# TensorE's order in a linear recurrence, written out for six of its eight pairs of heads

## The chip, the cores and the metric

The kernel runs on one core of a Trainium2 chip, as one program of some 42,600 instructions. The metric is the device time of one execution in microseconds; the table below has three timed runs and the profiled one. A core has five engines that are used here: TensorE (matmuls and transposes), VectorE, ScalarE, GpSimd and SyncE (which issues most transfers). Each goes through its own list of instructions in the order in which they were put there and waits on semaphores for the others.

## The reference

Three blocks of a network run one after the other on 512 tokens of width 1024: two attention layers, a block with a recurrence (RWKV) and a gated convolution, and a block with mLSTM and differential attention. All is in single precision; the kernel does each large matmul as three, from the high and low halves of both operands. The change lies in the second block:

```python
proj = h @ w_in                       # 1024 x 6400: r, k, v, low ranks, conv, gates
def step(S, inp):                     # one token; 16 heads of 64
    r_t, w_t, k_t, v_t, a_t, b_t = inp
    sa = einsum('bhij,bhj->bhi', S, a_t)
    S = S * w_t[:, :, None, :] + sa[..., None] * b_t[:, :, None, :] + v_t[..., None] * k_t[:, :, None, :]
    return S, einsum('bhij,bhj->bhi', S, r_t)
...
kk = kk / maximum(sqrt(sum(kk * kk)), 1e-12)      # per head
y = _rwkv7_scan(rh, decay, kh, vh, -kk, kk * ah)
y = (y - mean(y)) * rsqrt(var(y) + GN_EPS)        # per head
y_b = silu(layer_norm(conv1d(glu, conv_w, width 31) + conv_b))
merged = concatenate([(y + bonus) * g, y_b]) * sigmoid(gates)
x = x + gt_m * (merged @ w_out)
```

## The kernel before

`block2` is the second block. The 16 heads are worked in eight **pairs**, each on 128 partitions, and the 512 tokens in eight **chunks** of 64. For each pair p there are three parts.

`rwkv_prep` makes the operands: the low-rank decay and gates (`ps_w`, `ps_a`, `ps_cum`), the projections r, k, v (72 matmuls of 128x512 into `psg`, evicted as `xs_k`, `xs_r`, `xs_v`), the norm of each key column (`ps_kn`, the value `n`, an rsqrt by Newton steps on VectorE, `ps_kt`), then `kk`, `ar`, `kE`, the products within a chunk (`ps_M`, masked into four `MLR`) and transposes (`ps_kb`, `ps_vt`, `ps_bon`).

`rwkv_invert` inverts the triangular matrices of the chunks. Its 32x32 blocks go through DRAM to another layout (`dram_L`, then `uL`), VectorE inverts them in some 35 dependent steps (`uM`, `uT`, `uX`), the result comes back through DRAM (`dram_DT`, then `zD`), and TensorE puts the halves together (`ps_D`, `ps_T`, `ps_X`); ScalarE copies to `zD` and `XO` last.

`rwkv_steps` is the **chain** over the eight chunks. A chunk has three **hops** on TensorE: `ps_P<-S,ar` (copied by ScalarE to `VY`), the two `ps_u` (copied to `VU`), and `ps_s`, after which VectorE updates the state S in two instructions; two `ps_P<-VU,MLR` for the next chunk follow. Then come the outputs (16 `ps_y`), a normalisation per head on VectorE, GpSimd and ScalarE (GN), four transposes `ps_yt`, and Y goes to DRAM.

Beside that stand the **fillers**: the column tiles of the convolution (`conv_tiles`: matmuls, `glu`, and 30 **taps** on VectorE for each of eight tiles, into `z0` to `z7`) and of the gates (`gate_tiles`: matmuls and a sigmoid). Each column tile is 24 matmuls. A list `order` says which fillers are issued behind which pair: "c12" is convolution tiles 1 and 2, "g02" gate tiles 0 and 1.

The program is written in this order: prep and invert of pair 0; then for each pair its chain, prep and invert of the next pair, and the fillers of that pair at a lower priority. A scheduler lays out each engine's list from priorities and dependencies. Two lines bind it besides: the matmul `from_v` of a chunk comes after the last one of the chunk before, and the first tap of a convolution tile comes after the last step of the inversion that was issued last before the tile:

```python
inv = self.inv_last               # conv_tiles, when it is called
...
if j == 1:
    self.issue_after(tap, inv)
```

PSUM has four banks for `psg`, two for the preparation, and one each for `ps_u`/`ps_s` and `ps_P`. Weights come in slabs, which ScalarE rounds to their high half (`whi`) and VectorE or GpSimd subtract to the low half (`wlo`); in this stage one slab in three goes to VectorE.

## Time and profile before

| | |
|---|---|
| timed runs | 3638.11, 3644.20, 3645.26 us, median 3644.2 |
| profiled execution, its own time | 3647.22 us |
| its span, first to last instruction | 3645.4 us |
| mean granted TensorE clock | 0.929 |
| busy in the span: TensorE | 3261.1 us (89%) |
| VectorE | 2078.6 us (57%) |
| ScalarE | 1321.2 us (36%) |
| GpSimd | 522.7 us (14%) |

A share of busy time is a mean over stages with different limits. The granted clock is a share of 2.4 GHz; 0.5 is the lower of its two levels, 1.2 GHz. "Idle before" is how long an engine stood before an instruction, with what ended the wait.

### The profile page before, as it was taken

To read this page: it belongs to the slowest core of one execution; us is meant where nothing else is said; L and a number is where in the kernel's file an instruction comes from. 1 tells how busy PE (TensorE), PEld (TensorE's weight loads), DVE (VectorE), ACT (ScalarE), POOL (GpSimd) and SP (SyncE) were. 2 spreads that over 40 slices of the span, in tenths; PEclk is the share of its full clock that TensorE was granted. 3 is DMA by queue.
4 is the path that set the end of the run, shared out by engine and by line. 5 is a ranking of instruction groups with operands and counts; after the bars stand their busy time and mean duration, and the time that the engine had idled before them with its cause. 6 is when DMAs were issued, how large, how long until landed. Compare 5 with 4: busy or idle time off the path is not lost. (4 is left out here: it accounts for less than half of the span.)

```text
span 3645.4 us, 42576 instructions
## 1 busy us (share of the span) xinstructions
PE 3261.1 (89%) x15209; PEld 2559.2 (70%) x15209; DVE 2078.6 (57%) x3962; ACT 1321.2 (36%) x2472; POOL 522.7 (14%) x623
## 2 busy tenths in 40 slices
PE   8999999999999996785847766789999999999998
PEld 6666777887788875563635555678887777788887
DVE  4576654646653565665653834743336775566565
ACT  3465322334432342231222212433324454344344
POOL 1000010111110111220211212321101001101011
PEclk9999999999999997895866867899999999999999
DMA  4313554352233331110210213323333323433232
GB/s 145 97 58 99 160 163 139 125 144 74 78 98 98 99 103 42 54 53 14 61 40 26 59 40 119 107 85 98 95 97 90 102 64 110 144 99 99 93 95 84
DMA packets 275286, 332.64 MB, mean 91 GB/s; under 512 B 53212, under 2 KB 188314, under 8 KB 275073
## 3 DMA queue, kind: packets, MB, share of 16 engines
q1 hardware_dynamic: 237392, 301.43, 27.1%
q0 software_dynamic: 3936, 16.03, 1.4%
q10 hardware_dynamic: 33745, 12.46, 1.4%
q8 instruction: 120, 1.97, 0.2%
q14 instruction: 93, 0.76, 0.1%
HBM read 311.94 MB, written 23.89 MB: 92 GB/s over the span
## 5 line engine op out<-in xcount | busy, mean ns | idle before, releaser
L123 PE MATMUL psg<-hhi,whi 128*128 128x512 f32 (+1 forms) x2624 | 1049.3, 402 | 59.5 <-DVE glu L1318 27.4
L118 DVE TENSOR_TENSOR wlo<-raw,whi 128x512 fp32r<-128x512 f32 (+2 forms) x865 | 628.6, 738 | 795.2 <-PE psg L124 422.0
L125 PE MATMUL psg<-hhi,wlo 128*128 128x512 f32 (+1 forms) x2624 | 1046.3, 400 | 28.6 <-POOL wlo L118 15.5
L124 PE MATMUL psg<-hlo,whi 128*128 128x512 f32 (+1 forms) x2624 | 1047.5, 399 | 0.0
L117 ACT CAST whi<-raw 128x512 fp32r<-128x512 f32 (+2 forms) x975 | 582.6, 604 | 1196.1 <-PE psg L124 1031.3
L123 PEld LDWEIGHTS psg<-hhi,whi 128*128 128x128 f32 (+1 forms) x2624 | 500.9, 191 | 182.9 <-issue 29.4
L125 PEld LDWEIGHTS psg<-hhi,wlo 128*128 128x128 f32 (+1 forms) x2624 | 501.2, 191 | 141.4 <-POOL wlo L118 19.5
L124 PEld LDWEIGHTS psg<-hlo,whi 128*128 128x128 f32 (+1 forms) x2624 | 502.0, 191 | 104.7 <-issue 1.7
L123 PE MATMUL psg<-hidhi,whi 128*128 128x512 f32 x784 | 308.8, 394 | 2.1 <-DVE ffg L574 1.2
L125 PE MATMUL psg<-hidhi,wlo 128*128 128x512 f32 x784 | 307.5, 392 | 0.0
L124 PE MATMUL psg<-hidlo,whi 128*128 128x512 f32 x784 | 306.1, 390 | 0.0
L1322 DVE SCALAR_TENSOR_TENSOR z<-glu,par_B,z 128x512 f32<-128x512 f32 x240 | 185.2, 800 | 3.3
L118 POOL TENSOR_TENSOR wlo<-raw,whi 128x512 fp32r<-128x512 f32 (+1 forms) x110 | 139.0, 1272 | 286.7 <-ACT whi L117 202.8
L125 PEld LDWEIGHTS psg<-hidhi,wlo 128*128 128x128 f32 x784 | 147.2, 188 | 34.3
L123 PEld LDWEIGHTS psg<-hidhi,whi 128*128 128x128 f32 x784 | 147.4, 188 | 34.0 <-issue 1.6
L124 PEld LDWEIGHTS psg<-hidlo,whi 128*128 128x128 f32 x784 | 147.3, 188 | 32.9
L581 POOL TENSOR_TENSOR ffu<-ffu,ffg 128x512 f32<-128x512 f32 x44 | 64.6, 1469 | 587.9 <-DVE ffu L574 587.9
L1273 DVE SCALAR_TENSOR_TENSOR S<-S,GC,ps_s 64x64 f32<-64x64 f32 x112 | 31.3, 280 | 130.0 <-PE ps_s L1271 128.5
L1391 POOL TENSOR_TENSOR ffr<-ffr 128x512 f32<-128x512 f32 x32 | 40.1, 1261 | 293.8 <-ACT ffr L1390 288.9
L1212 PE MATMUL ps_D<-ident,zD 128*128 128x128 f32 x32 | 7.9, 394 | 82.0 <-DMA zD<-dram_DT 82.0
L194 ACT CAST hidhi<-ffu 128x512 fp32r<-128x512 f32 x66 | 41.0, 622 | 106.1 <-POOL ffu L581 66.2
L195 DVE TENSOR_TENSOR hidlo<-ffu,hidhi 128x512 fp32r<-128x512 f32 x66 | 57.3, 868 | 30.9 <-ACT hidhi L194 29.4
(576 smaller groups left out, 4174.8 us busy)
## 6 DMA issues: line engine op xcount, KB each, us to landing
raw<-in_ffn_w_gu_dram SPq DMA_DIRECT2D x176, 256.0 KB
raw<-in_w_in_dram SPq DMA_DIRECT2D x59, 512.0 KB
adraw<-in_ada_w_dram SPq DMA_DIRECT2D x48, 512.0 KB
raw<-in_w_up_dram SPq DMA_DIRECT2D x88, 256.0 KB
raw<-in_ffn_w_down_dram SPq DMA_DIRECT2D x42, 512.0 KB
raw<-in_w_ff_in_dram SPq DMA_DIRECT2D x32, 512.0 KB
...
```

Of the source, the lines that this page charges most:

```text
L117: nc.scalar.copy(oi(hi), ri(r))
L118: eng.tensor_tensor(out=oi(lo), in0=ri(r), in1=fr(oi(hi)), op=ALU.subtract)
L123: first = nc.tensor.matmul(ps, lhsT=whi, rhs=xhi, start=start, stop=False)
L124: nc.tensor.matmul(ps, lhsT=whi, rhs=xlo, start=False, stop=False)
L125: nc.tensor.matmul(ps, lhsT=wlo, rhs=xhi, start=False, stop=stop)
L194: nc.scalar.copy(hi, t)
L195: nc.vector.tensor_tensor(out=lo, in0=t, in1=fr(hi), op=ALU.subtract)
L581: nc.gpsimd.tensor_tensor(out=t, in0=t, in1=part[c], op=ALU.mult)
L1212: nc.tensor.transpose(ps[:, c * 128:(c + 1) * 128], DT[:, 2 * c:2 * c + 2, :].rearrange("p c t -> p (c t)"), self.ident)
L1273: nc.vector.scalar_tensor_tensor(out=S[h, h], in0=S[h, h], scalar=GC[h, c:c + 1], in1=pss[h, h], op0=ALU.mult, op1=ALU.add)
L1322: tap = nc.vector.scalar_tensor_tensor(out=z[i], in0=g[:, j:j + T], scalar=cw(j), in1=z[i], op0=ALU.mult, op1=ALU.add)
L1391: nc.gpsimd.tensor_tensor(out=t, in0=t, in1=t, op=ALU.mult)
```

## The change

Matmuls and transposes go through two helpers, `mm` and `tp`, which record them in named segments. The order of issue in `block2` is another: `rwkv_prep` is cut in two (the first half is `ps_w` to the projections, the second the rest), `rwkv_steps` in three (chain; outputs and GN; `ps_yt`), all as generators. For pair p now come the chain of p, the outputs of p-1, the second half of the preparation of p+1, the `ps_yt` of p-1, the fillers of p, the first half of the preparation of p+2, and the inversion of p+1. For pairs 0 to 5 `in_turn` then gives TensorE's order in full: it lists fillers and preparation in a fixed sequence, gives each matmul a weight, and puts the 24 hops of the chain in at equal distances in these weights. All recorded matmuls behind pair 5 come after the end of that list. VectorE, ScalarE, GpSimd and the transfers keep the scheduler's order. Fillers are spread anew over the pairs, `VY` gets a second buffer, and `bon` lies in other buffers.

```diff
-            order = ["c01", "c12", "c31 g02", "c42", "g22", "c62 g41", "g51 h01", "g62 h13 n h44 x p y04 n2 q r y43 m08 s", "x yw y7 w"]
+            order = ["c01 g02", "c12", "c31 g22", "c42", "c61 g42", "c71 g62", "h04", "n h44 x p y04 n2 q r y43 m08 s", "x yw y7 w"]
...
-            P = self.rwkv_prep(W, act, 0, low)
-            self.rwkv_invert(P)
-            for f in order[0].split():
-                filler(f)
-            for p in range(8):
-                low["y7"] = self.rwkv_steps(P, y_d)
-                if p < 7:
-                    P = self.rwkv_prep(W, act, p + 1, low)
-                    self.rwkv_invert(P)
+            def fill(p):
+                self.seg("F", p)
                 for f in order[p + 1].split():
                     filler(f)
+            prep = {p: self.rwkv_prep(W, act, p, low) for p in range(8)}
+            next(prep[0])
+            P = next(prep[0])
+            next(prep[1])
+            self.rwkv_invert(P)
+            fill(-1)
+            end, steps = None, {}
+            for p in range(8):
+                steps[p] = self.rwkv_steps(P, y_d)
+                for q in {6: (6, 5, 5, 6, 6), 7: (7, 7, 7)}.get(p, (p, p - 1)):
+                    if q >= 0:
+                        low["y7"] = next(steps[q])
+                if p < 7:
+                    P = next(prep[p + 1])
+                if 0 < p < 6:
+                    next(steps[p - 1])
+                fill(p)
+                if p < 6:
+                    next(prep[p + 2])
+                if p < 7:
+                    self.rwkv_invert(P)
+                if p < 6:
+                    end = self.in_turn(p, end)
...
+    def in_turn(self, p, end):
+        g = lambda *n: [(i, {"w": 0.25, "G": 0.23, "F": 0.23, "kn": 0.12, "kt": 0.11, "M": 0.1, "D": 0.11, "T": 0.06, "X": 0.06,
+                             "y": 0.1, "yt": 0.1}[n[0]]) for i in self.segs.get(n, [])]
+        F, G = g("F", p), g("G", p + 2)
+        cut = lambda l, us: (l[:int(us / 0.23)], l[int(us / 0.23):])
+        f0, F = cut(F, 1.5)
+        f1, F = cut(F, 4.0)
+        f2, F = cut(F, 8.0)
+        f3, F = cut(F, 4.0)
+        G, g2 = G[:-14], G[-14:]
+        B = (g("y", p - 1) + f0 + g("kn", p + 1) + f1 + g("kt", p + 1) + f2 + g("M", p + 1) + f3 + g("yt", p - 1) + F + g("w", p + 2) + G +
+             g("D", p + 1) + g2[:7] + g("T", p + 1) + g2[7:] + g("X", p + 1))
+        step = sum(w for _, w in B) / 24
+        out, t, k = [], 0.0, 0
+        for i, w in B:
+            while k < 24 and t >= step * k:
+                out += self.segs.get(("C", p, k), [])
+                k += 1
+            out.append(i)
+            t += w
...
+        for a, b in zip(([end] if end is not None else []) + out, out if end is not None else out[1:]):
+            self.issue_after(b, a)
+        return out[-1]
```

What this moves, first on TensorE around the `ps_D` of the second preparation. Rows are line, operation, output and inputs, size; `hhi` and `hlo` are the activations' halves, and the number of `zD` tells even and odd pairs apart (10969 is an odd pair's). Before:

```order
L124 MATMUL psg<-hlo_10768,whi 128x512
L125 MATMUL psg<-hhi_10767,wlo 128x512
L123 MATMUL psg<-hhi_10773,whi 128x512
L1212 MATMUL ps_D<-ident,zD_10969 128x128 x4
L124 MATMUL psg<-hlo_10774,whi 128x512
L125 MATMUL psg<-hhi_10773,wlo 128x512
L123 MATMUL psg<-hhi_10779,whi 128x512
L1218 MATMUL ps_T<-D,zC 32x32 x16
L124 MATMUL psg<-hlo_10780,whi 128x512
L125 MATMUL psg<-hhi_10779,wlo 128x512
L123 MATMUL psg<-hhi_10785,whi 128x512
L1226 MATMUL ps_X<-zD_10969,zT 32x32 x16
```

Before, `ps_D`, `ps_T` and `ps_X` of a pair (here pair 1) stand among fillers, and no hop of a chain lies between them. After, around the `ps_D` of pair 2:

```order
L130 MATMUL ps_P<-S,ar 128x128
L130 MATMUL psg<-hhi_10797,wlo 128x512
L130 MATMUL psg<-hhi_10803,whi 128x512
L136 MATMUL ps_D<-ident,zD_10968 128x128 x4
L130 MATMUL psg<-hlo_10804,whi 128x512
L130 MATMUL psg<-hhi_10803,wlo 128x512
L130 MATMUL psg<-hhi_10797,whi 128x512
L130 MATMUL psg<-hlo_10798,whi 128x512
L130 MATMUL psg<-hhi_10797,wlo 128x512
L130 MATMUL ps_u<-VY,zD_10969 64x64
L130 MATMUL ps_u<-VY,XO 64x64
L130 MATMUL psg<-hhi_10803,whi 128x512
```

The `psg` here are projections of pair 3, and hops of the chain of pair 1 (`ps_P<-S,ar`, then `ps_u` from `zD_10969`) stand before and behind the `ps_D` of pair 2.

The second place is the start of a preparation on TensorE. Before, behind the chain of pair 1:

```order
L123 MATMUL psg<-hhi_10779,whi 128x512
L1298 MATMUL ps_yt<-ident,Y 128x128 x4
L1054 MATMUL ps_w<-WD,tw 128x128 x4
L124 MATMUL psg<-hlo_10780,whi 128x512
L125 MATMUL psg<-hhi_10779,wlo 128x512
L123 MATMUL psg<-hhi_10785,whi 128x512
L1059 MATMUL ps_a<-alo,WA 128x512
L1064 MATMUL ps_cum<-tri,sT 128x128 x4
```

After the transposes of pair 1's output come `ps_w`, `ps_a` and `ps_cum` of pair 2, and its projections follow. After, behind the last step (`ps_X`) of pair 2's preparation:

```order
L130 MATMUL ps_P<-VU,MLR 128x64
L130 MATMUL ps_P<-S,ar 128x128
L130 MATMUL ps_y<-VU,MLR 64x64 x16
L130 MATMUL psg<-hhi_10761,whi 128x512
L130 MATMUL psg<-hlo_10762,whi 128x512
L130 MATMUL psg<-hhi_10761,wlo 128x512
L130 MATMUL ps_u<-VY,XO 64x64
L130 MATMUL ps_u<-VY,zD_10968 64x64
L130 MATMUL psg<-hhi_10767,whi 128x512
L130 MATMUL psg<-hlo_10768,whi 128x512
L130 MATMUL psg<-hhi_10767,wlo 128x512
L130 MATMUL ps_kn<-bones,kksq 128x2 x4
```

The chain of pair 2 begins, the outputs of pair 1 and six fillers with a hop between follow, and then `ps_kn` of pair 3; `ps_w` and the projections of pair 3 have stood ahead.

The third is VectorE in the last steps of an inversion. Before, of pair 1; `z_10973` and `z_10974` are the convolution's tiles 1 and 2, so rows with them are taps:

```order
L1173 TENSOR_REDUCE uX<-uT 128x6x8
L1172 TENSOR_TENSOR uT<-uX,uL 128x384
L1173 TENSOR_REDUCE uX<-uT 128x2x8
L1172 TENSOR_TENSOR uT<-uX,uL 128x256
L1173 TENSOR_REDUCE uX<-uT 128x2x8
L1172 TENSOR_TENSOR uT<-uX,uL 128x128
L1173 TENSOR_REDUCE uX<-uT 128x2x8
L1172 TENSOR_TENSOR uT<-uX,uM 128x512
L1173 TENSOR_REDUCE uX<-uT 128x8x8
L1322 SCALAR_TENSOR_TENSOR z_10973<-glu,par_B,z_10973 128x512
L118 TENSOR_TENSOR wlo<-raw,whi 128x384
L1322 SCALAR_TENSOR_TENSOR z_10973<-glu,par_B,z_10973 128x512 x6
```

The steps follow each other, and the taps stand behind the last. After, in the inversion of pair 2, with the taps of tile 3 (L1248 and L1249 are the steps that were L1172 and L1173):

```order
L1248 TENSOR_TENSOR uT<-uX,uM 128x384
L1409 SCALAR_TENSOR_TENSOR z_10975<-glu,par_B,z_10975 128x512
L1249 TENSOR_REDUCE uX<-uT 128x6x8
L1409 SCALAR_TENSOR_TENSOR z_10975<-glu,par_B,z_10975 128x512
L1248 TENSOR_TENSOR uT<-uX,uL 128x384
L1409 SCALAR_TENSOR_TENSOR z_10975<-glu,par_B,z_10975 128x512
L1249 TENSOR_REDUCE uX<-uT 128x2x8
L1409 SCALAR_TENSOR_TENSOR z_10975<-glu,par_B,z_10975 128x512
L1248 TENSOR_TENSOR uT<-uX,uL 128x256
L1356 SCALAR_TENSOR_TENSOR S<-S,GC,ps_s 64x64 x2
L1249 TENSOR_REDUCE uX<-uT 128x2x8
```

Each step has a tap behind it.

## Rows read from the trace of the kernel before

**Rows 1.** The page's slices: busy tenths of TensorE, and the TensorE clock granted, in 40 equal slices of 91.1 us; the sixteenth slice begins at 1367 us.

```profile
PE   8999999999999996785847766789999999999998
...
PEclk9999999999999997895866867899999999999999
```

**Rows 2.** Busy time of each engine in stretches: start:end and length, then busy us of TensorE's matmuls, its weight loads, VectorE, ScalarE and GpSimd (instructions in brackets), the mean granted clock, the busy share of the DMA engines, GB/s. The first is the recurrence, the second runs from the first ps_u of pair 0 to that of pair 6, the third from that of pair 7 to the next block's ps_sum.

```profile
1360.00:2320.00 960.00, 663.29 (x3534) 506.71 (x3533) 548.63 (x1083) 252.16 (x515) 183.56 (x234) 0.77 0.19 55
...
1434.57:2155.55 720.98, 486.86 (x2652) 374.62 (x2652) 422.91 (x832) 184.05 (x377) 141.93 (x189) 0.77 0.16 44
...
2286.42:2423.63 137.21, 116.12 (x521) 91.05 (x521) 85.29 (x138) 48.72 (x88) 50.72 (x37) 0.86 0.31 96
...
2320.00:2350.00 30.00, 15.37 (x84) 12.01 (x83) 29.66 (x42) 15.04 (x23) 22.18 (x15) 0.74 0.31 98
```

**Rows 3.** TensorE in order of time, start and duration in us; in brackets the idle time before it and what ended it: the first ps_u of pair 0; the steps of pair 1's preparation; the first ps_u of pair 1; the first of pair 6.

```profile
1434.57 0.33 PE L1267 MATMUL ps_u<-VY,XO 64*64 64x64 f32 x2 [1.14 <-ACT XO L1232]
...
1472.33 1.11 PE L1298 MATMUL ps_yt<-ident,Y 128*128 128x128 f32 x4 [8.47 <-POOL Y L1295]
...
1481.22 1.05 PE L1084 MATMUL ps_kn<-bones,kksq 128*128 128x2 f32 x8 [1.70 <-ACT kksq L1081]
...
1547.52 1.05 PE L1212 MATMUL ps_D<-ident,zD 128*128 128x128 f32 x4
...
1551.45 1.10 PE L1226 MATMUL ps_X<-zD,zT 128*32 128x32 f32 x32
...
1553.84 0.32 PE L1267 MATMUL ps_u<-VY,XO 64*64 64x64 f32 x2
...
2155.55 0.47 PE L1267 MATMUL ps_u<-VY,XO 64*64 64x64 f32 x2 [1.14 <-ACT XO L1232]
```

**Rows 4.** VectorE in order of time in the same preparation, of pair 1: the column norm (n), its use (kk), the four MLR, the inversion's first step (uM) and last (uX).

```profile
1482.31 0.17 DVE L1087 TENSOR_SCALAR n<-ps_kn 128x8 f32<-128x8 f32 x1 [0.17 <-PE ps_kn L1084]
...
1490.07 0.69 DVE L1097 TENSOR_TENSOR kk<-kk,ps_kt 128x512 f32<-128x512 f32 x1 [1.45 <-PE ps_kt L1096]
...
1496.31 1.29 DVE L1117 TENSOR_TENSOR MLR<-ps_M,maskM 128x512 f32<-128x512 f32 x2 [1.31 <-PE ps_M L1114]
...
1498.64 1.29 DVE L1117 TENSOR_TENSOR MLR<-ps_M,maskM 128x512 f32<-128x512 f32 x2 [1.04 <-PE ps_M L1114]
...
1515.63 1.13 DVE L1178 COPY uM<-uL 128x256 f32<-128x256 f32 x1 [6.85 <-POOL uL L1162]
...
1532.24 0.69 DVE L1173 TENSOR_REDUCE uX<-uT 128x64 f32<-128x512 f32 x1
```

**Rows 5.** Who waited for whom in 1360 to 2320 us: us in total, times, longest.

```profile
PE ps_D L1212 <- DMA zD<-dram_DT: 82.0, 5, 29.7
...
PE ps_yt L1298 <- POOL Y L1295: 69.9, 7, 17.7
...
PE ps_P L1262 <- DVE S L1273: 9.3, 25, 1.1
...
DVE uM L1178 <- POOL uL L1162: 65.6, 8, 10.0
```

**Rows 6.** TensorE in order of time: two matmuls of the projections, 128x512, that follow each other at the lower clock, and two at the full one; the distance of their starts is what one costs.

```profile
1586.73 0.63 PE L125 MATMUL psg<-hhi,wlo 128*128 128x512 f32 x1
...
1587.15 0.63 PE L123 MATMUL psg<-hhi,whi 128*128 128x512 f32 x1
...
1591.31 0.40 PE L123 MATMUL psg<-hhi,whi 128*128 128x512 f32 x1
...
1591.54 0.39 PE L124 MATMUL psg<-hlo,whi 128*128 128x512 f32 x1
```

**Rows 7.** TensorE and VectorE in order of time, other pairs: ps_D of pair 0; the last uX and the ps_D of pair 2; ps_w and ps_kn, the last uX and the ps_D of pair 7.

```profile
1428.07 1.09 PE L1212 MATMUL ps_D<-ident,zD 128*128 128x128 f32 x4 [7.53 <-DMA zD<-dram_DT]
...
1659.02 0.69 DVE L1173 TENSOR_REDUCE uX<-uT 128x64 f32<-128x512 f32 x1
...
1667.84 1.09 PE L1212 MATMUL ps_D<-ident,zD 128*128 128x128 f32 x4 [29.08 <-DMA zD<-dram_DT]
...
2195.19 1.91 PE L1054 MATMUL ps_w<-WD,tw 128*128 128x128 f32 x8
...
2202.70 1.05 PE L1084 MATMUL ps_kn<-bones,kksq 128*128 128x2 f32 x8 [2.08 <-ACT kksq L1081]
...
2262.92 0.69 DVE L1173 TENSOR_REDUCE uX<-uT 128x64 f32<-128x512 f32 x1
...
2279.32 0.76 PE L1212 MATMUL ps_D<-ident,zD 128*128 128x128 f32 x4
```

**Rows 8.** VectorE's groups by line in 1360 to 2320 us (count | busy us, mean ns | idle before, and whom it waited for): the taps of the convolution and the update of the state. The mean of a tap counts pieces twice that overlap; 185.2 us for 240 is 0.77.

```profile
L1322 DVE SCALAR_TENSOR_TENSOR z<-glu,par_B,z 128x512 f32<-128x512 f32 x240 | 185.2, 800 | 3.3
...
L1273 DVE SCALAR_TENSOR_TENSOR S<-S,GC,ps_s 64x64 f32<-64x64 f32 x112 | 31.3, 280 | 130.0 <-PE ps_s L1271 128.5
```

**Rows 9.** VectorE in order of time: two steps of small rsqrt chains on 128x4 and 128x8, the first beside an idle GpSimd, the second while the convolution is normalised.

```profile
2318.46 0.16 DVE L255 TENSOR_TENSOR rs_t<-rs_t,rs_h 128x4 f32<-128x4 f32 x1
...
2341.39 1.23 DVE L255 TENSOR_TENSOR rs_t<-rs_t,rs_h 128x8 f32<-128x8 f32 x1
```

**Rows 10.** TensorE in order of time in pair 7's chain: the first ps_u of two chunks that follow each other with no filler between.

```profile
2290.47 0.47 PE L1267 MATMUL ps_u<-VY,zD 64*64 64x64 f32 x2 [0.35 <-ACT VY L1263]
...
2294.57 0.47 PE L1267 MATMUL ps_u<-VY,XO 64*64 64x64 f32 x2 [0.35 <-ACT VY L1263]
```

More of the change, by code (lines that the diff above doesn't have):

```diff
@@ L122, in mm3, with mm, tp, seg @@
         nc = self.nc
-        first = nc.tensor.matmul(ps, lhsT=whi, rhs=xhi, start=start, stop=False)
-        nc.tensor.matmul(ps, lhsT=whi, rhs=xlo, start=False, stop=False)
-        nc.tensor.matmul(ps, lhsT=wlo, rhs=xhi, start=False, stop=stop)
-        return first
+        first = self.mm(ps, lhsT=whi, rhs=xhi, start=start, stop=False)
+        self.mm(ps, lhsT=whi, rhs=xlo, start=False, stop=False)
+        self.mm(ps, lhsT=wlo, rhs=xhi, start=False, stop=stop)
+        return first
+    def mm(self, *a, **k):
+        i = self.nc.tensor.matmul(*a, **k)
+        if self.rec is not None:
+            self.rec.append(i)
+        return i
+    def tp(self, *a, **k):
+        i = self.nc.tensor.transpose(*a, **k)
+        if self.rec is not None:
+            self.rec.append(i)
+        return i
+    def seg(self, *name):
+        self.rec = None if name == (None,) else self.segs.setdefault(name, [])
     def issue_after(self, ins, earlier):
@@ L234, in colsum @@
                 first = i == 0 and b == 0
-                self.sum_ins = nc.tensor.matmul(ps[:, 0:8] if first else ps[:, b * 2:b * 2 + 2],
+                self.sum_ins = self.mm(ps[:, 0:8] if first else ps[:, b * 2:b * 2 + 2],
                                                 lhsT=ss[:, b * 128:(b + 1) * 128],
@@ L395, in toeplitz_table @@
             ps = self.ps("s", "ps_t")
-            nc.tensor.matmul(ps[0:nh, 0:w], lhsT=t, rhs=oh, start=True, stop=True)
+            self.mm(ps[0:nh, 0:w], lhsT=t, rhs=oh, start=True, stop=True)
             nc.vector.scalar_tensor_tensor(out=o, in0=ps[0:nh, 0:w], scalar=-1.0, in1=ad, op0=ALU.mult, op1=ALU.subtract)
@@ L480, in sc @@
                 def sc(e, qb, ps):
-                    nc.tensor.matmul(ps, lhsT=qz[2 * m + e][:, qb * 128:(qb + 1) * 128], rhs=kt[m], start=True, stop=True)
+                    self.mm(ps, lhsT=qz[2 * m + e][:, qb * 128:(qb + 1) * 128], rhs=kt[m], start=True, stop=True)
                 po = self.ps("o", "ps_pv")
@@ L542, in sc @@
                 def sc(e, qb, ps):
-                    nc.tensor.matmul(ps, lhsT=qh[2 * m + e][:, qb * 128:(qb + 1) * 128], rhs=kh[2 * m + e], start=True, stop=True)
+                    self.mm(ps, lhsT=qh[2 * m + e][:, qb * 128:(qb + 1) * 128], rhs=kh[2 * m + e], start=True, stop=True)
                 po = self.ps("o", "ps_pv")
@@ new lines, in block2 @@
+            self.lo_on = "v"
+            self.seg(None)
+            late = [i for n, l in self.segs.items() for i in l if (n[0] in ("C", "F") and n[1] > 5) or (n[0] in ("y", "yt") and n[1] >= 5)
+                    or (n[0] in ("kn", "kt", "M", "D", "T", "X") and n[1] > 6)]
+            for i in late:
+                self.issue_after(i, end)
+            rst.close()
+    def in_turn(self, p, end):
[18 more added lines that the diff above has]
+            t += w
+        while k < 24:
+            out += self.segs.get(("C", p, k), [])
+            k += 1
+        for a, b in zip(([end] if end is not None else []) + out, out if end is not None else out[1:]):
+            self.issue_after(b, a)
+        return out[-1]
@@ L1050, in rwkv_prep @@
         got = {}
+        self.seg("w", p)
         ps = self.psp("ps_w")
         for b in range(NB):
-            nc.tensor.matmul(ps[:, b * 128:(b + 1) * 128], lhsT=low["w"][:, b * 128:(b + 1) * 128], rhs=WD,
+            self.mm(ps[:, b * 128:(b + 1) * 128], lhsT=low["w"][:, b * 128:(b + 1) * 128], rhs=WD,
                              start=True, stop=True)
@@ L1058, in rwkv_prep @@
         ps = self.psp("ps_a")
-        nc.tensor.matmul(ps, lhsT=WA, rhs=low["a"], start=True, stop=True)
+        self.mm(ps, lhsT=WA, rhs=low["a"], start=True, stop=True)
         at = self.rot("a")
@@ L1077, in rwkv_prep @@
         r, k, v = got["r"], got["k"], got["v"]
+        yield
+        self.seg("kn", p)
         kk = self.rot("kk")
@@ L1141, in rwkv_prep @@
         ps = self.psp("ps_bon")
-        nc.tensor.matmul(ps, lhsT=self.bones, rhs=t, start=True, stop=True)
-        bon = self.sp.tile([128, T], F32, tag="RSTD", name="bon", bufs=2) if p % 3 == 2 else self.rp.tile([128, T], F32, tag="bon", name="bon", bufs=2)
+        self.mm(ps, lhsT=self.bones, rhs=t, start=True, stop=True)
+        bon = self.sp.tile([128, T], F32, tag="RSTD", name="bon", bufs=2) if p % 3 else self.rp.tile([128, T], F32, tag="bon", name="bon")
         nc.vector.tensor_tensor(out=bon, in0=ps, in1=v, op=ALU.mult)
-        return dict(p=p, Ld=Ld, ar=arc, KB=KB, VU=VU, MLR=MLR, MLRc=MLRc, GC=GC, bon=bon)
+        yield dict(p=p, Ld=Ld, ar=arc, KB=KB, VU=VU, MLR=MLR, MLRc=MLRc, GC=GC, bon=bon)
     def cdma(self, **kw):
@@ L1257, in from_v @@
                 self.issue_after(i, last[0])
-            nc.tensor.matmul(psP[:, c % 4, up], lhsT=MLRc[:, 1, c], rhs=VU[:, c, up], start=False, stop=False)
+            self.mm(psP[:, c % 4, up], lhsT=MLRc[:, 1, c], rhs=VU[:, c, up], start=False, stop=False)
+        self.seg("C", p, 0)
         from_v(0)
         for c in range(8):
-            last[0] = nc.tensor.matmul(psP[:, c % 4, :], lhsT=ar[:, c], rhs=S, start=False, stop=True)
+            self.seg("C", p, 3 * c)
+            last[0] = self.mm(psP[:, c % 4, :], lhsT=ar[:, c], rhs=S, start=False, stop=True)
             nc.scalar.copy(VY[:, c, :], psP[:, c % 4, :])
             own = halves[1 - c % 2]
+            self.seg("C", p, 3 * c + 1)
             psu = self.ps("st", "ps_u")
             for e, h in enumerate(halves):
-                nc.tensor.matmul(psu[up, h], lhsT=XT(e, c), rhs=VY[own, c, h], start=True, stop=True)
+                self.mm(psu[up, h], lhsT=XT(e, c), rhs=VY[own, c, h], start=True, stop=True)
             nc.scalar.copy(VU[up, c, :], psu[up, 0:128])
+            self.seg("C", p, 3 * c + 2)
             if c < 7:
                 pss = self.ps("st", "ps_s")
-                nc.tensor.matmul(pss[:, 0:128], lhsT=KB[:, c, :], rhs=VU[:, c, :], start=True, stop=True)
+                self.mm(pss[:, 0:128], lhsT=KB[:, c, :], rhs=VU[:, c, :], start=True, stop=True)
                 for h in halves:
@@ L1279, in rwkv_steps @@
                 for q in range(2):
-                    nc.tensor.matmul(psy[halves[q], b, h], lhsT=MLR[up, e, b, 3 * q, :], rhs=VU[up, 2 * b + q, h], start=True, stop=True)
+                    self.mm(psy[halves[q], b, h], lhsT=MLR[up, e, b, 3 * q, :], rhs=VU[up, 2 * b + q, h], start=True, stop=True)
         for q, h in enumerate(halves):
```

83 lines of the change are left out of this document (47 added, 36 removed).

## The prediction

> **What bounds the kernel now.** I read the slices of the page first: TensorE is full almost everywhere but in a dip of ten slices, where its granted clock falls too [rows 1]. The stretches say how large the dip is: 1360 to 2320 us, 960 us, in which TensorE is busy 663 us at a mean clock of 0.77, VectorE 549 us, and no other engine half as long [rows 2]. No engine bounds this stage; a loop does. Its period is read from the first ps_u of each pair's chain: 1434.57 for pair 0, 2155.55 for pair 6, so 721.0 us for six pairs, 120.2 us each [rows 3].
>
> One round of the loop, from pair 0 to pair 1, read from the instructions of VectorE and TensorE in order of time [rows 3, 4]: chain and its output 1434.6 to 1472.3 (ps_yt), projections from there to 1481.2 (ps_kn), then the column norm, n at 1482.31 to kk at 1490.07 (7.8 us), kk to the first MLR 6.2, the four MLR to 1499.93 (3.6), a trip through DRAM to uM at 1515.63 (15.7), the inversion to the end of the last uX, 1532.93 (17.3), a second trip to ps_D at 1547.52 (14.6), ps_D to the end of ps_X 5.0, and the next chain at 1553.84. All of it is one after the other: the chain of pair p, then the preparation of p+1. Who waits confirms it: TensorE stands 82.0 us before ps_D and 69.9 us before ps_yt, and the inversion's start on VectorE, uM, waits 65.6 us in eight pairs for uL [rows 5]. The big matmuls ("fillers") that stand behind ps_D and ps_yt on TensorE wait with them.
>
> **The change part by part.** *Wrapping matmuls in a helper, recording them:* no instruction. *The order for pairs 0 to 5:* the chain of pair p now runs beside the preparation of p+1, hop by hop, and the projections of p+2 fill the time before ps_D. This removes from the loop the chain, GN and projections, 1434.6 to 1481.2, 46.6 us a round. What is left, X to X: end of ps_X to the norm, with the 16 ps_y, a few fillers and ps_kn ahead of it, 5 us (1.3 us to the first ps_u in [rows 3, 4], 1.1 for ps_kn, the rest fillers); norm 8; kk to MLR 11, since 34 fillers of 0.23 us [rows 6] and two hops now stand before ps_M; MLR 3.6; first trip 17 (15.7 here, where uM waited 6.85 us; the mean wait is 65.6 / 8 = 8.2 [rows 4, 5]); inversion 17; second trip 8.5 (14.6 and 15.7 where TensorE came late, 8.1 where ps_D itself waited for the transfer [rows 4, 7]); D to X 7 (5.0, and 14 fillers between). Sum 77 us.
>
> *VectorE's order, which nobody wrote out:* the taps of the convolutions (L1322 before, L1409 after) were tied behind the inversion last issued. The fillers are now issued before `rwkv_invert` of the next pair, so they hang on the inversion before it, and the order of after shows them between the steps of the norm and of the inversion. I counted there, between n and kk and between uM and the last uX: 24, 32, 10, 31, 13 and 0 taps in pairs 0 to 5, 110 in all; besides them 38 updates of S, 15 wlo and 5 Y inside the inversions. A tap costs 0.77 us (185.2 us for 240; 0.69 where two chains of taps alternate [rows 8]): 85 us; S 38 x 0.28 = 11, wlo and Y (0.7 to 0.8 each) 14 beyond the two evictions that the measured inversion holds: 110 us by mean durations. Means of overlapping instructions count too much: by them the six rounds hold 475 us of VectorE, while six pairs of before, with 15 taps (12 us) fewer, hold 422.9 busy [rows 2], so I scale by 435 / 475 = 0.92 to 101 us. Bounds: nothing, if all taps fell into the trips; 130 if neighbouring GpSimd work stretches the steps (a small step that takes 0.16 us takes 1.2 in one spot [rows 9]).
>
> *Pairs with few taps:* there TensorE's own list from ps_M to ps_D, 97 fillers and 12 hops, is 22 us of fillers at the full clock, 42 at half [rows 6], beside 17 + 17 + 8.5 = 42 of trip, inversion, trip. The mean clock of before was 0.77; with four chunks of the chain between them, at up to 4.1 us [rows 10], the list can come out later at half clock. I put 5 us on each of three pairs, 15 (bounds 0 and 45).
>
> *Hand-overs:* seven times a pair VectorE stops at S for TensorE, and TensorE at the next ps_P for S. At equal distances in the fillers both usually have work; 2 us a pair, 12 (bounds: nothing, and rival 3).
>
> Six rounds: 6 x 77 + 101 + 15 + 12 = 590 us for 721.0, a gain of 131.
>
> *Before and after the six pairs:* ahead of ps_D of pair 0 stand 130 fillers behind ps_M where 87 stood; 43 more, 9.9 us at full and 18.5 at half clock, against 7.53 us that TensorE waited there [rows 6, 7]: +5 (bounds 2 and 11). From pair 6's chain to pair 7's: the projections (ps_w 2195.19 to ps_kn 2202.70, 7.5 us [rows 7]) have been done: -7. Work behind it: 387 fillers before the next norm's ps_sum, 385 after, so this stretch (137.2 us [rows 2]) keeps its length, but for the normalisation of the convolution, which now stands before the last chain on VectorE; in 2320 to 2350 TensorE was busy 15.4 of 30 us while VectorE did it [rows 2, 9]: -5 (bounds 0 and -15).
>
> *Extra buffers (VY doubled, bon moved):* memory only. *Two halves of a preparation at once in the rotating buffers:* the second half of pair p+1 has read its tiles by ps_M, before the first half of p+2 is issued; nothing.
>
> The sum against the profiled execution: 3647.2 - 131 + 5 - 12 = 3509 us. That execution stands 3.0 us above the median, 3644.2, so I forecast 3506.
>
> The two trips weigh 25 us in each round, so their price matters. The row: from the last MLR to uM 15.7 us, from the last uX to ps_D 8.1 at the least. The Trainium skill ("DMA: Bandwidth & Descriptors", Anatomy of one DMA) gives about 2 us of fixed cost for a transfer; a trip is a write and a read, so by it some 4 us, an estimate, and the sum would fall by about 17 us a round, to some 3404. No trip in this trace is that short, and the measurement decides.
>
> **The rivals.**
> 1. *The engines bound it.* If taps fall into the trips and waits are hidden, a round is what an engine has to do. TensorE: 486.9 busy in six pairs, 81 a round at the mean clock of 0.77, about 62 if the clock stays full [rows 2]. VectorE: 435 / 6 = 73. Then 6 x 73 = 438, a gain of 283: about 3355. For it: no count of work stands in the way. Against: it asks for all seven transfers and three VectorE runs of a round to lie beside other pairs' work, while pair p+1 must be inverted within p's round. Halfway to it lies 3430.
> 2. *The inversion under taps is no shorter than what was removed.* If each small step beside a tap pays for GpSimd too (upper bound 130), the second trip is 14.6, and the low-clock term is 45: 462 + 130 + 37 + 45 + 12 = 686, a gain of 35; with +11 and -7 for what lies around them, 3647 - 35 + 4 = 3616, beside the median 3613. For it: GpSimd's 142 us of work in these rounds [rows 2] gets denser.
> 3. *Slower: the hand-overs are paid in full.* Two engines that keep their order and meet seven times a pair: if each meeting costs the bare round of a chunk, 4.1 us [rows 10], on top of the rest, that is 28.7 a pair, 172 for six, instead of 12: 3506 + 160 = 3666, slower by 22. It decides from 3.6 us a meeting (138 / 42 = 3.3, and 0.3 counted already). Against: TensorE's waits for S were 9.3 us over 25 times before [rows 5], and the hops are spread in the list. For it: that order is kept is plain where TensorE stood up to 29.7 us before ps_D with fillers behind it [rows 5]. The Trainium skill ("TensorE: Matmul & The Clock Gate", Architectural detail) says of VectorE that it is a strict first-in-first-out queue and of TensorE that only weight loads are pulled ahead; by that rule a meeting that is missed is never worked around, and the time is the 3666 of this rival. The trace agrees as far as these waits go.
> 4. *No change:* the removed 46.6 us come back as some 44 in each round; only a mixture of 2 and 3 does that.
>
> **How the numbers follow.** My forecast, with its own range 3440 to 3575: 0.68. Rival 1 and its neighbourhood below 3440: 0.14. Rival 2, 3575 to 3637: 0.10. Rival 4: 0.02. Rival 3: 0.06. The terms' bounds give the range: all low (0 for taps is rival 1; half of 101, no low clock, no hand-over) 3647 - 721 + 513 - 20 = 3419; all high is rival 2. I leave out some 0.1 on each side: 3440 to 3585. Differences of 0.2% (7 us) are about what measurements of this kernel tell apart: faster 0.91, same 0.02, slower 0.07.
>
> **What would show it.** The first ps_u of pairs 0 to 6 should lie 75 to 112 us apart, longest in pairs 1 and 3, shortest in pair 5; if all are alike near 73, rival 1. uM to the last uX should take 28 to 39 us in pairs 0 to 4 and 17 to 20 in pair 5. The wait before ps_yt should vanish and one before ps_D or ps_kt remain. If ps_P and S head the list of waits, rival 3. The clock of the stage should stay under 0.9. The prediction is wrong if taps don't lengthen the inversion, or if TensorE stops for something I gave no price: an eviction, a wlo, or ScalarE held at the issue of a transfer that waits for the inversion, with chain hops behind it.

## The result, and the profile after

The changed kernel takes 3486.4 us (median of four runs, 3485.4 to 3487.9) beside 3644.7 for the kernel before (3640.8 to 3645.3 in the series below): ratio 0.9569, 95% interval 0.9552 to 0.9585. The forecast was 3506 with 3440 to 3585 around it; the gain is 158 us where 138 was expected. The profiled execution took 3487.93 us, its span 3486.1.

The page's slices of the changed kernel, as [rows 1]; the stage that begins in the sixteenth slice is shorter, and its clock higher:

```profile
PE   8999999999999998777768784999999999999998
...
PEclk9999999999999999788978885999999999999999
```

The stretches, as [rows 2], same columns: from the first ps_u of pair 0 to that of pair 6, from there to that of pair 7, and on to the next block's ps_sum:

```profile
1438.62:2019.56 580.94, 444.42 (x2659) 342.81 (x2659) 414.76 (x826) 186.30 (x376) 151.66 (x184) 0.86 0.21 58
2019.56:2141.01 121.45, 67.84 (x406) 52.09 (x405) 70.96 (x169) 36.26 (x71) 28.53 (x24) 0.73 0.31 91
2141.01:2265.40 124.39, 116.93 (x508) 91.44 (x508) 51.38 (x93) 36.23 (x69) 37.38 (x29) 0.89 0.28 89
```

The six rounds take 580.9 us where they took 721.0 [rows 2]; VectorE has nearly the same work in them (414.8 us busy, 422.9 before), and TensorE the same matmuls, at a mean granted clock of 0.86 instead of 0.77. The next two stretches were 130.9 and 137.2 [rows 2, 3].

TensorE in order of time, as [rows 3]: the first ps_u of pairs 0 to 7. The rounds are 97.8, 106.9, 88.4, 109.0, 92.5 and 86.4 us; the last one, from pair 6 to 7, which the list doesn't cover, is 121.5.

```profile
1438.62 0.47 PE L130 MATMUL ps_u<-VY,XO 64*64 64x64 f32 x2
1536.40 0.33 PE L130 MATMUL ps_u<-VY,XO 64*64 64x64 f32 x2
1643.31 0.32 PE L130 MATMUL ps_u<-VY,XO 64*64 64x64 f32 x2
1731.69 0.32 PE L130 MATMUL ps_u<-VY,XO 64*64 64x64 f32 x2
1840.71 0.33 PE L130 MATMUL ps_u<-VY,XO 64*64 64x64 f32 x2
1933.16 0.32 PE L130 MATMUL ps_u<-VY,XO 64*64 64x64 f32 x2
2019.56 0.33 PE L130 MATMUL ps_u<-VY,XO 64*64 64x64 f32 x2
2141.01 0.33 PE L130 MATMUL ps_u<-VY,XO 64*64 64x64 f32 x2 [1.14 <-ACT XO L1311]
```

One round as VectorE and TensorE see it, the preparation of pair 2, as [rows 4] showed that of pair 1:

```profile
1538.57 0.17 DVE L1161 TENSOR_SCALAR n<-ps_kn 128x8 f32<-128x8 f32 x1 [0.90 <-PE ps_kn L130]
...
1553.22 0.69 DVE L1172 TENSOR_TENSOR kk<-kk,ps_kt 128x512 f32<-128x512 f32 x1
...
1587.24 1.05 DVE L1254 COPY uM<-uL 128x256 f32<-128x256 f32 x1 [4.15 <-POOL uL L1238]
...
1622.20 0.67 DVE L1249 TENSOR_REDUCE uX<-uT 128x64 f32<-128x512 f32 x1
...
1630.99 1.09 PE L136 MATMUL ps_D<-ident,zD 128*128 128x128 f32 x4 [12.96 <-DMA zD<-dram_DT]
```

The norm, n to kk, takes 14.7 us (7.8 in [rows 4]), the inversion 35.6 (17.3): 9 taps stand in the one and 23 in the other. Then the second trip: 8.1 us, for which TensorE waits.

Who waited in 1360 to 2320 us, as [rows 5]. The wait before ps_yt, 69.9 us, is 4.9; ps_D's is 49.5 instead of 82.0; ps_kt's, for VectorE's norm, has grown from 4.5 to 30.5, and ps_P's, for S, from 9.3 to 26.8:

```profile
PE ps_D L136 <- DMA zD<-dram_DT: 49.5, 6, 13.0
DVE uM L1254 <- POOL uL L1238: 48.0, 8, 7.9
PE ps_kt L136 <- ACT kksq L1167: 30.5, 7, 7.6
PE ps_P L130 <- DVE S L1356: 26.8, 16, 4.3
...
PE ps_yt L136 <- POOL Y L1380: 4.9, 3, 2.3
```

### The profile page after: what moved, and what is told of

Its sections match the earlier page's. It is cut to its first block, busy times and chain, and to the rows that moved or that the text cites. A ratio compares the mean times of both kernels' runs of the same rounds, so it can differ in the third digit from the quotient of the medians.

```text
span 3486.1 us, 42525 instructions
## 1 busy us (share of the span) xinstructions
PE 3202.7 (92%) x15209; PEld 2518.7 (72%) x15209; DVE 2050.3 (59%) x3961; ACT 1324.3 (38%) x2470; POOL 534.0 (15%) x622
## 5 line engine op out<-in xcount | busy, mean ns | idle before, releaser
L130 PEld LDWEIGHTS psg<-hhi,whi 128*128 128x128 f32 (+1 forms) x2624 | 501.2, 191 | 149.0 <-issue 12.6
L119 POOL TENSOR_TENSOR wlo<-raw,whi 128x512 fp32r<-128x512 f32 (+2 forms) x109 | 147.2, 1357 | 313.5 <-ACT whi L118 202.7
L782 DVE SCALAR_TENSOR_TENSOR adacc<-adraw,c_act,adacc 128x1024 f32<-128x1024 f32 x42 | 53.9, 1283 | 32.3 <-DMA adraw<-in_ada_w_dram 32.1
L226 POOL TENSOR_TENSOR ss<-ss,sq 128x512 f32<-128x512 f32 x24 | 35.6, 1484 | 217.3 <-ACT sq L225 201.5
```

Source lines behind the costliest of these rows:

```text
L119: eng.tensor_tensor(out=oi(lo), in0=ri(r), in1=fr(oi(hi)), op=ALU.subtract)
L130: i = self.nc.tensor.matmul(*a, **k)
L226: (nc.gpsimd if c < 4 else nc.vector).tensor_tensor(out=ss, in0=ss, in1=sq, op=ALU.add)
L782: nc.vector.scalar_tensor_tensor(out=acc, in0=raw, scalar=c[:, k:k + 1], in1=acc, op0=ALU.mult, op1=ALU.add)
```

## The experiments

**The taps.** *few_taps*:

```diff
-            for j in range(1, 31):
+            for j in range(1, 3):
                 tap = nc.vector.scalar_tensor_tensor(out=z[i], in0=g[:, j:j + T], ...)
```

> The changed kernel with two of the 30 taps of each convolution tile (j = 1, 2); the other 28 are left out, and nothing else is touched. Theory, the taps lie on the path: of the changed kernel's six rounds (97.8, 106.9, 88.4, 109.0, 92.5, 86.4 us, 580.9 in all) the norm (n to kk) and the inversion (uM to last uX) take 65.7 and 169.8; without taps the shortest of each are 7.3 and 18.4, so 44 + 110: the rounds fall by 81 to about 500, are alike (80 to 87 each), and the time is 3486 - 81 = 3405. Rival, TensorE's own list at the low clock binds in their place: ps_D no longer waits for zD, the rounds fall by less than 40, time above 3446.

Measured: 3407.0 us (one run). The stretch of the six rounds, and the inversion of pair 2:

```profile
1435.25:1935.14 499.89, 420.05 (x2660) 325.67 (x2659) 260.31 (x603) 184.54 (x377) 134.12 (x183) 0.94 0.24 68
```

```profile
1553.56 1.05 DVE L1254 COPY uM<-uL 128x256 f32<-128x256 f32 x1 [7.81 <-POOL uL L1238]
...
1571.05 0.69 DVE L1249 TENSOR_REDUCE uX<-uT 128x64 f32<-128x512 f32 x1
...
1584.37 0.60 PE L136 MATMUL ps_D<-ident,zD 128*128 128x128 f32 x4
```

Six rounds in 499.9 us, 81.0 less; the inversion is 18.2, and ps_D now comes 12.6 us after it without a wait: the transfer (8.1) is no longer last, TensorE's own list is, in five of the six preparations. So the rival's sign came too, but not its time. Of the 110 taps that lay in norm and inversion 8 are left there, and these two fell by 71 us (235.4 to 164.3), 0.70 us a tap. The other 10 us are a balance: the steps from kk to MLR, MLR and ps_D to ps_X are 22 us shorter, at a mean granted clock of 0.94 instead of 0.86, and the second trip is 12 longer because TensorE comes late to ps_D. The stretch from the last MLR to ps_D in this preparation:

```profile
1539.97:1584.37 44.40, 36.90 (x187) 28.25 (x188) 21.00 (x50) 14.99 (x32) 8.55 (x16) 0.96 0.29 82
```

**The distances of the hops.** *bursts*:

```diff
-            while k < 24 and t >= step * k:
+            while k < 24 and t >= step * (k - k % 3):
```

> The changed kernel with the three hops of a chunk put in together, at eight places instead of 24. Theory, the equal distances hide the hand-overs: each hop behind the first then waits for the copy or for S, a chunk costs TensorE up to its bare 4.1 us less 0.3, 8 x 6 x 3.8 = 182 at the most; since ps_D and ps_kt wait anyway (49.5 and 30.5 us), a part is covered: slower by 60 to 180, 3546 to 3666. Rival, the distances don't matter because VectorE's norm and inversion set the round: less than 20 slower, under 3506.

Measured: 3515.9 us (one run), 29.5 slower; neither expectation. TensorE's waits from 1432 to 2049 us, of this kernel:

```profile
PE ps_u L130 <- ACT VY L1344: 56.6, 47, 10.9
...
PE ps_s L130 <- ACT VU L1350: 16.0, 42, 1.1
...
PE ps_D L136 <- DMA zD<-dram_DT: 3.8, 2, 2.6
```

Nearly every one of the 48 chunks does wait for its copies, 72.6 us in all, but of the changed kernel's waits for zD (43.5 in these limits) and for S (25.8) nearly nothing is left: what TensorE loses at the hops it would have lost at ps_D. The six rounds of *bursts*:

```profile
1432.62:2048.67 616.05, 469.54 (x2673) 373.35 (x2673) 416.76 (x825) 186.14 (x377) 141.43 (x184) 0.82 0.20 55
```

TensorE stands 146.5 us in them, 10 more than in the changed kernel, and is busy 25 us longer with the same matmuls, at 0.82 of its clock instead of 0.86: most of what the distances are worth, 0.6 us a chunk, shows as clock and not as waiting.

**List or program order.** *no_list* leaves out the list:

```diff
-                if p < 6:
-                    end = self.in_turn(p, end)
...
-            for i in late:
-                self.issue_after(i, end)
```

> The changed kernel without the list of TensorE's order (in_turn is not called): only the new order of issue in the program, and the scheduler lays out TensorE. Theory, the list makes the gain: the scheduler lets the chain stand in front again, more than half of the gain is lost, 3565 or more. Rival, the gain comes from the program's order (preparation cut in two, two pairs ahead): within 20 us of 3486.

*one_ahead* is that, and the two halves of a preparation together again:

```diff
-            next(prep[1])
...
+                    next(prep[p + 1])
                     P = next(prep[p + 1])
...
-                if p < 6:
-                    next(prep[p + 2])
```

> The kernel without the list (no_list, 3503.1), and with both halves of the preparation of p+1 issued together behind the chain of p, as before the change; the outputs of p still come a pair later. Theory, preparing two pairs ahead takes the projections (8.9 us from ps_yt to ps_kn in the kernel before) out of each of six rounds: 54 us slower than no_list, about 3557. Rival, the projections find room beside the chain anyway, since the preparation needs nothing of it: within 15 us of 3503.

*own_outputs* is no_list with the outputs behind their own chain:

```diff
-                for q in {6: (6, 5, 5, 6, 6), 7: (7, 7, 7)}.get(p, (p, p - 1)):
+                for q in (p, p, p):
...
-                if 0 < p < 6:
-                    next(steps[p - 1])
```

> The kernel without the list (no_list, 3503.1), with the outputs, GN and ps_yt of pair p issued right behind its own chain instead of a pair later; the halved preparation and the two pairs ahead stay. Theory, what kept chain and preparation apart was that the PSUM banks of the preparation (two, in rotation) came round behind ps_y and ps_yt of the same pair, which need the whole chain: ps_kn then waits for the chain and GN again, 34 + 5 us or more in each of six rounds, 200 to 280 slower, but no slower than the kernel before by more than its projections gain: 3600 to 3700. Rival, halving the preparation and running it ahead is enough: under 3545.

Measured, one run each: 3503.1, 3499.8 and 3608.3 us. The theory of the list fell: without it some 140 of the 158 us are still there, within the 20 us that its rival gave. no_list, from the end of pair 0's preparation to the start of pair 1's, and its six rounds:

```profile
1444.11 1.10 PE L130 MATMUL ps_X<-zD,zT 128*32 128x32 f32 x32
1445.14 1.06 PE L130 MATMUL ps_kn<-bones,kksq 128*128 128x2 f32 x8
```

```profile
1447.40:2038.03 590.63, 473.43 (x2739) 364.17 (x2738) 427.30 (x828) 191.21 (x391) 162.45 (x188) 0.81 0.23 65
```

The preparation starts at once without the list too. How much of the other 17 us is the list's is not shown: no_list was run once, its granted clock was 0.94 over the first 1360 us too, where the changed kernel had 0.99, and it enters the recurrence 6.0 us later (n of pair 0 at 1369.26 and 1363.24). Preparing two pairs ahead, the mechanism that the rival named, shows no gain without the list either (one_ahead is 3.3 us faster than no_list). Putting the outputs back behind their own chain costs 105 us; own_outputs keeps 36 us of the gain over the kernel before, and its projections still come two pairs ahead. TensorE in order of time in own_outputs, the end of pair 0's preparation and the start of pair 1's:

```profile
1437.92 1.10 PE L130 MATMUL ps_X<-zD,zT 128*32 128x32 f32 x32
1442.73 0.32 PE L130 MATMUL ps_y<-VU,MLR 64*64 64x64 f32 x2
...
1468.85 0.44 PE L130 MATMUL ps_y<-VU,MLR 64*64 64x64 f32 x6
1489.96 0.65 PE L136 MATMUL ps_yt<-ident,Y 128*128 128x128 f32 x4 [4.18 <-POOL Y L1374]
1490.45 1.42 PE L130 MATMUL ps_kn<-bones,kksq 128*128 128x2 f32 x8
```

The first ps_y comes 4.8 us behind ps_X, the last after the chain; ps_kn, which needs neither, stands right behind ps_yt, 52.5 us after ps_X.

**The banks.** ps_y, ps_yt, ps_D, ps_T, ps_X and all other tiles of the preparation but its projections come from the same two PSUM banks, in the order of the program. *own_bank* is own_outputs, *before_bank* the kernel before, each with only this:

```diff
-        psy = self.ps("p", "ps_y").rearrange("p (b m) -> p b m", b=NB)
+        psy = self.ps("st", "ps_y").rearrange("p (b m) -> p b m", b=NB)
...
-        ps = self.ps("p", "ps_yt")
+        ps = self.ps("st", "ps_yt")
```

> own_outputs (3608.3: no list, the outputs of p right behind its own chain), with ps_y and ps_yt in the bank of ps_u and ps_s instead of the two that the preparation uses. Theory, the rotation of these two banks is what holds ps_kn and all behind it back until the chain and GN are through (41 to 53 us from ps_X to n in each round, against 5 to 8 in no_list): with it gone the preparation starts at once, and the time comes within 25 us of no_list, 3480 to 3530. Rival, it is the scheduler's priorities, or buffers of the outputs (VY, Y, bon) that keep them apart: it stays above 3590.

> The kernel before with nothing but that edit: ps_y and ps_yt in the bank of ps_u and ps_s. Theory, the loop loses chain and GN as in the changed kernel (46.6 us a round without the list), and gets the next preparation's projections, which stood behind the banks as well; its taps stay behind the inversion but fall into the norm in part, as in one_ahead: 90 to 150 faster, 3495 to 3555. Rival, the order of issue (outputs and chain ahead of the preparation) keeps them apart: above 3610.

Measured: own_bank 3465.4 us (one run), before_bank 3449.5 (two runs, 3445.4 and 3453.7; ratio 0.9466, 0.9437 to 0.9495). Both are faster than the lower end of what was expected (3480 and 3495), and neither rival is left. Two lines in the kernel before are worth more than the whole change. The same place on TensorE, first in the kernel before, then in before_bank:

```profile
1431.80 1.62 PE L1226 MATMUL ps_X<-zD,zT 128*32 128x32 f32 x32 [0.45 <-ACT zT L1222]
...
1435.78 0.33 PE L1280 MATMUL ps_y<-VU,MLR 64*64 64x64 f32 x2
...
1473.24 1.92 PE L1054 MATMUL ps_w<-WD,tw 128*128 128x128 f32 x8
```

```profile
1429.99 1.73 PE L1226 MATMUL ps_X<-zD,zT 128*32 128x32 f32 x32 [0.45 <-ACT zT L1222]
1431.65 2.08 PE L1054 MATMUL ps_w<-WD,tw 128*128 128x128 f32 x8
...
1442.01 0.95 PE L1084 MATMUL ps_kn<-bones,kksq 128*128 128x2 f32 x8
...
1464.08 1.15 PE L1280 MATMUL ps_y<-VU,MLR 64*64 64x64 f32 x32
...
1476.71 0.66 PE L1298 MATMUL ps_yt<-ident,Y 128*128 128x128 f32 x4 [0.83 <-POOL Y L1295]
```

Before, the first ps_y took one of the two banks at 1435.78 and held it to the end of the chain; ps_yt is next in the rotation, and ps_w of the next pair followed it (1472.33 in [rows 3]). With ps_y elsewhere ps_w and ps_kn come 41.6 and 39.2 us earlier, ahead of ps_y. The six rounds take 573.5 us:

```profile
1435.36:2008.85 573.49, 431.02 (x2654) 327.82 (x2653) 426.49 (x830) 184.65 (x376) 144.86 (x188) 0.87 0.20 55
```

**Versions.** *taps_in_trips* is the changed kernel with one convolution tile per pair and each tile's taps `l` tied between preparations (the two tiles of pair 5 only at their start; the gate tiles are spread anew beside them):

```diff
+                self.issue_after(l[0], self.ux[p + 1])
+                    self.issue_after(self.n8[p + 2], l[17])
+                    self.issue_after(l[18], self.mlr[p + 2])
+                    self.issue_after(self.um[p + 2], l[-1])
```

> The changed kernel with one convolution tile per pair (pairs -1 to 4, two in pair 5), and its 30 taps tied: 18 between the last uX of one preparation and the n of the next, 12 between the last MLR and uM. Theory, as for few_taps: the norm returns to 7.3 us and the inversion to 18 to 20 in each round, 81 less; VectorE waits 4 to 8 us for uL in each first trip, so 12 taps of 0.77 lengthen it by 2 to 5 at most: six rounds 500 to 530, time 3405 to 3435. Rival, VectorE's other work (evictions, Y, wlo) comes late behind 18 taps and n with it: gain under 30, above 3456.

*seven_pairs* is the changed kernel with the list for one pair more; *seven_taps* has both edits:

```diff
-                if p < 6:
+                if p < 7:
                     end = self.in_turn(p, end)
+                if p == 6:
+                    next(steps[6]), next(steps[6])
+                    fill("tail")
```

> The changed kernel with the list for seven pairs: the chain of pair 6 runs beside the second half of the preparation of pair 7, whose outputs and the convolution's normalisation come behind it. Theory, the stretch from the first ps_u of pair 6 to that of pair 7 (121.5 us, in which TensorE is busy 68) falls to a round without taps, 85 to 95, and the 124 us behind it keep their length since TensorE is busy 117 of them: 27 to 36 faster than the changed kernel, 3450 to 3460. Rival, the normalisation of the convolution (ps_sum of zs at 2086, of zss at 2116 us, both inside that stretch) is pushed behind pair 7's chain and the last matmuls wait for it: 3476 to 3496 or slower.

> taps_in_trips (3423.6) with the list for seven pairs. Theory, the two edits add up: its stretch from pair 6 to pair 7 is 134.3 us and falls to 90 to 100 (the two tiles of pair 5 are still in it), 3380 to 3390. Rival, as for seven_pairs, the normalisation binds the end: 3410 or more.

Measured: 3423.6 us (3414 to 3437; ratio 0.9389, 0.9366 to 0.9413), 3465.2 (0.9513, 0.9493 to 0.9534) and 3411.0 (0.9361, 0.9342 to 0.9380). The stretches, of taps_in_trips (six rounds) and of seven_pairs (pair 6 to 7, then to the next ps_sum):

```profile
1439.32:1961.27 521.95, 431.09 (x2659) 334.69 (x2659) 410.11 (x792) 184.83 (x375) 134.79 (x182) 0.91 0.23 65
```

```profile
2014.12:2096.94 82.82, 53.97 (x364) 42.89 (x365) 40.92 (x100) 20.92 (x46) 14.16 (x13) 0.79 0.38 115
2096.94:2239.50 142.56, 120.72 (x557) 94.86 (x556) 90.23 (x162) 52.22 (x93) 54.91 (x40) 0.89 0.30 93
```

The same taps, out of norm and inversion, give back 59 of the 81 us. In seven_pairs the seventh round falls by 38.6 us, more than expected, but the normalisation behind it lengthens the end by 18.2, as the rival said: a gain of 21, between the two expectations. Both edits together are 12.5 us better than taps_in_trips, not the 21 of seven_pairs and short of the 34 to 44 expected; 3411.0 is what the rival gave. The stretch behind the first ps_u of pair 7, to the next block's ps_sum, in taps_in_trips, and the last two stretches of seven_taps:

```profile
2095.57:2214.61 119.04, 112.47 (x508) 88.48 (x508) 51.70 (x91) 34.43 (x66) 35.46 (x28) 0.92 0.28 90
```

```profile
1945.06:2036.55 91.49, 54.41 (x365) 42.48 (x365) 64.95 (x131) 21.53 (x47) 18.49 (x15) 0.79 0.34 102
2036.55:2176.79 140.24, 117.78 (x556) 92.55 (x555) 90.91 (x164) 52.10 (x93) 54.89 (x40) 0.91 0.31 97
```

The step from pair 6 to 7 came down as expected, to 91.5 us; the end is 21.2 longer, as in seven_pairs. The profiled executions lie 36 us apart (3436.7, the slowest of its kernel, and 3400.7, the fastest), so these rows do not add up to the medians.

*bank_taps* puts such ties on before_bank, *seven_even* spreads the taps of seven_taps evenly over seven rounds:

```diff
+            for q, n in enumerate((30, 30, 36, 36, 36, 36, 36), 1):
+                l, i = taps[i:i + n], i + n
+                self.issue_after(l[0], self.ux[q - 1])
+                self.issue_after(self.n8[q], l[17])
+                self.issue_after(l[18], self.mlr[q])
+                self.issue_after(self.um[q], l[-1])
```

> before_bank (3449.5) with the taps tied as in taps_in_trips, and spread evenly: 30 or 36 in each of seven rounds, 18 of them between the last uX of a preparation and the next n, the rest between the last MLR and uM. Theory, in before_bank the norm (n to kk) takes 113 us in the seven rounds and the inversion 145, where 8 and 18.4 a round would be 56 and 129; 73 less, given back in part by first trips that grow by up to 3 us each: 35 to 70 faster, 3380 to 3415. Rival, TensorE's own work binds once the rounds are near 85: under 15 faster, above 3435.

> seven_taps (3411.0) with its taps spread evenly in the same way over seven rounds, where two tiles stood behind pair 5. Theory, the last two rounds (92.1 and 91.5 us, with an inversion of 28.0 and a norm of 15.5) come down to the 80 to 85 of the others: 10 to 18 faster, 3393 to 3401. Rival, TensorE's list sets these rounds too: within 5 of 3411.

Measured: 3437.5 us (0.9431, 0.9410 to 0.9453) and 3420.9 (0.9385, 0.9366 to 0.9405): 12 better than before_bank instead of 35 or more, which is the time that the rival gave (the two intervals overlap), and 10 worse than seven_taps, neither expectation. VectorE in seven_even: its taps between pair 6's last MLR and its uM (count | busy us, mean ns | idle before), and this uM in order of time:

```profile
L1421 DVE SCALAR_TENSOR_TENSOR z<-glu,par_B,z 128x512 f32<-128x512 f32 x25 | 19.3, 808 | 0.3
```

```profile
1922.23 0.28 DVE L1266 COPY uM<-uL 128x256 f32<-128x256 f32 x1
```

uM starts without a wait, 23.2 us behind the last MLR, against 14.3 in seven_taps: 25 taps are more than the trip holds. Twelve were not (15.0 us at most in taps_in_trips). By the edit there can be more than the 18 of the ties, since a round's share spans two tiles here and the ties hold only the later one. In bank_taps the norm did fall, to 8.8 to 11.9 us, but its first trips grew to between 16.7 and 22.3, and two inversions took 25 and 31 with 12 and 14 taps in them. In four of its seven preparations ps_D came without a wait for the transfer, 10.1 to 15.7 us behind the last uX, so there TensorE's own list was last, as the rival has it.

## Why the prediction was right, and where it was not

**The time** came out because the sum of the rounds was nearly right. Its terms were less so: five rows are 48 us over, three are 58 under, and that these cancel is luck. Forecast and measured, us over six rounds (ps_X to ps_X):

| | forecast | measured |
|---|---|---|
| ps_X to n | 30 | 31.9 |
| norm, inversion and VectorE's order in them | 48 + 102 + 101 = 251 | 65.7 + 169.8 = 235.5 |
| kk to MLR | 66 | 82.9 |
| the four MLR | 22 | 28.8 |
| first trip | 102 | 86.0 |
| second trip | 51 | 59.4 |
| ps_D to the end of ps_X | 42 | 56.2 |
| low clock, hand-overs | 15 + 12 | in the rows above |
| sum | 590 | 581 |

*VectorE's order* was the term that mattered, and its mechanism is shown: 24, 32, 10, 31, 13 and 0 taps stand in norm and inversion, as forecast, and without 102 of them the two are 71 us shorter and the rounds 81.0, where 78 of the 101 were theirs (85 x 0.92). The other 23, for S, wlo and Y, were too much: the inversion of pair 5, with no tap in it, took 18.4 where 17 was assumed for all. (The 0.69 us for a tap where two chains alternate is not in [rows 8], and no sum uses it.) The forecast signs came: rounds between 86 and 109, longest in pairs 1 and 3, shortest in pair 5; inversions of 26.1 to 35.6 and then 18.4 (26.9, 26.1 and 27.8 lie just under the stated 28).

*Trips.* Where TensorE waits for the second it takes 8.1 to 8.3 us, as in [rows 7], or 9.6 and 9.7 (pairs 3 and 1). The first was 14.3 on average, not 17, and uM waited for uL in it, as before; why it is shorter was not tried. By the Trainium skill ("DMA: Bandwidth & Descriptors", Anatomy of one DMA) each would have been some 4 us, an estimate; that section is on transfers that GpSimd issues, and ScalarE issues these. No kernel here shows a trip under 8.0 us, and the measurement decides.

*Low clock and hand-overs* were 27, and more than that came, in other rows: kk to MLR, MLR and ps_D to ps_X together are 38 us over their terms, since hops of the chain and fillers stand between their steps on TensorE; that this is the cause was read from the order, not tested. At pair 5 ps_D came without a wait 15.6 us behind the last uX, 7 over the second trip's 8.5: there TensorE's list was last, in one pair of the three for which that was priced. The clock is not the reason that was given for it: the granted clock was 0.86 from the last MLR to this ps_D, and in few_taps the list is last in five of six preparations at 0.94. The list itself was priced too short, with 22 us of fillers at the full clock; few_taps shows 44.4 us of it at 0.96, TensorE busy for 36.9. In *bursts*, with the hops three together, the waits for the copies are 1.5 us a chunk and the time grows by 0.6 a chunk, not by the 3.6 a meeting from which rival 3 decides: TensorE had slack at ps_D.

*Around the rounds*: the first ps_u of pair 0 is 4.1 us later (5); pair 6 to 7 is 9.4 shorter (7), the stretch behind 12.8 shorter (5). With 140.0 for 131 in the rounds that makes 158.

**The step that failed is the cause**, though the time was right. The prediction said of the order for pairs 0 to 5, the list, that it removes chain, GN and projections from the loop, 46.6 us a round. The list is not needed for that: no_list has the overlap too, and one_ahead has it without projections two pairs ahead. What let chain and preparation overlap is that the outputs of a pair are issued a pair later, so that ps_y and ps_yt no longer take the preparation's two banks before it: own_outputs undoes this, at 105 us, and own_bank gets the overlap back by another bank alone. The prediction read from the order of events that the preparation comes after the chain and took it for a dependency, though no value passes from one to the other. Of the buffers it asked only whether the new order would wait for them, not whether the old one did. By no_list the list itself is worth at most 17 us, and before_bank shows that the whole is not needed. The Trainium skill ("Perfetto Trace Analysis", Optimization Strategy) says that the same gap repeating on an engine that should be full can mean that there isn't enough SBUF or PSUM for the next tile to be allocated. The rows agree: the gap before ps_yt came in seven of eight rounds, 69.9 us [rows 5], and with ps_y and ps_yt in one other bank 12.4 us of it are left.

Why before_bank beats the changed kernel by 37 us is mostly seen: its step from pair 6 to 7 takes 88.1 us, where the other's is 121.5. In the changed kernel the outputs of pair 6 come right behind its own chain, in the preparation's banks, and from ps_X to the next n it takes 43.8 us there, where the kernel before takes 49 to 58. own_bank confirms it: its six rounds are as long as those of no_list (591.3 and 590.6), and this step falls from 120.0 us to

```profile
2029.26:2123.68 94.42, 44.52 (x282) 34.24 (x281) 59.23 (x139) 27.97 (x58) 21.28 (x16) 0.59 0.23 64
```

The six rounds of before_bank are 7.4 us shorter besides; what its fewer taps in the inversions and the scheduler's order on TensorE are worth in them was not tried apart.
